# Decoding two tiles' experts inside the expert loop, with own pools for the first product's operands

## The chip, the cores and the metric

The kernel runs on one core of a Trainium2 chip. The metric is the device time of one execution in microseconds (us), lower is better. A core has engines that run their own instruction lists in order and meet by semaphores: TensorE (PE, matrix products), VectorE (DVE), ScalarE (ACT), GpSimd (POOL) and SyncE (SP, which here only issues transfers). Transfers are moved by 16 DMA engines, whichever engine issued them.

## The reference, cut to what matters

One encoder layer over 1024 tokens of width 1024: attention, a layer norm, and then a layer of product-key experts (PEER), to which the change belongs:

```python
q   = (x @ w_q).reshape(n, 8, 2, 128)
sc  = einsum('nhpc,hpkc->nhpk', q, sub_keys)          # 8 heads x 2 halves x 128 keys
s_top, i_top = top_k(sc, 16)
cand     = s_top[:, :, 0, :, None] + s_top[:, :, 1, None, :]
cand_idx = i_top[:, :, 0, :, None] * 128 + i_top[:, :, 1, None, :]
fs, fpos = top_k(cand, 16);  eidx = take(cand_idx, fpos);  g = softmax(fs)
h   = einsum('cd,chkd->chk', x, u[eidx])              # 16384 experts, one row of u and of v each
out = einsum('chk,chkd->cd', gelu(h) * g, v[eidx])
x   = layer_norm(alpha * x + out)
```

Every token uses 8 x 16 = 128 of 16384 experts.

## The kernel before, in words

The 1024 tokens are eight tiles of 128. Attention and routing take the tiles in pairs: `route(pr)`, for tiles 2pr and 2pr+1, forms the scores on PE, takes each half's best 16 on DVE (`top16`) and then calls `decode`, some 150 small DVE instructions per tile that turn 2 x 16 scores per head into 16 expert numbers and 16 gate values.

From there two ways lead to the output. Tiles 0 to 4 (`ND` = 5) go the dense way: their gates are written as a matrix over all 16384 experts, and h and the output are dense products. For tiles 0 and 1 the gates are added into memory by 256 indirect transfers that POOL issues one after the other (`scatter`, L165; memory tensor `gs`). For tiles 2 to 4 `build` makes them: DVE writes one-hot rows (`pi`, `qj`, L602 and L606), ACT scales `qj` (L611), PE multiplies them (L615), ACT copies the product into a staging tile (L616) and SP writes that to memory tensor `gd` (L617). Tiles 5 to 7 go the gathering way: POOL fetches for one expert slot the 128 rows of u and v that 128 tokens need (`uv`, L656); DVE multiplies and sums them with the tokens (`xg`, L658), ACT applies gelu, DVE multiplies with the gate (`hh`, L663) and adds the scaled v row to `acc` (L668). There are 384 such gathers.

After the routing (`late.close()` frees its buffers) comes the expert loop of 128 blocks of 128 experts. Per block `hstage` loads a block of u, splits it into a rounded part and a rest (`uh` on ACT, `ul` on DVE), makes h in two halves of 24 products each (L91 to L93), applies gelu (`gl`), multiplies with the gates (`gt`, L722), splits that (`ah`, `al`) and splits a block of v (`vh`, `vl`). The output is summed in PSUM for tiles 0 to 2 (`po`, 18 products per block) and, every second block, flushed for tiles 3 and 4 (`fl`, `facc`). The loop also feeds the gathers: three per block, four blocks' worth ahead.

The order of every engine's list is fixed when the program is built: a scheduler places instructions of different stages beside each other where data and buffers allow. A pool of tiles that opens later can lie on memory that an earlier pool has given back; its first writer then waits for the last users of what lay there.

Of the kernel before, what the change touches and what calls it, by code (L numbers as in the profile page):

```python
# [11 lines left out]
F32 = mybir.dt.float32  # L12
F32R = mybir.dt.float32r
BF16 = mybir.dt.bfloat16
I32 = mybir.dt.int32
U32 = mybir.dt.uint32
# [3 lines left out]
PSUM = bass.MemoryType.PSUM  # L20

P = 128
S = 1024
D = 1024
KT = D // P
# [6 lines left out]
TOPK = 16  # L32
# [7 lines left out]
DN = ND * P  # L40
# [17 lines left out]
def trunk(ctx, tc, x, xt, wqk, wo, gn, sink, biasa, biasb, ln, wq, keyst, uv, ut, vt, out):  # L58
    nc = tc.nc
    f = lambda ap: ap.bitcast(F32)  # L60
# [20 lines left out]
    def load_ln(g):  # L81
        for i in range(2):
            nc.scalar.dma_start(lnt[:, i, :], bcast_rows(ln[2 * g + i], D))
# [89 lines left out]
            new.append(st.ins)  # L173
        added[t, h] = new

    def decode(idx, g, sv, iv, pool, t=None):
        s2 = sv.rearrange("p (h two) k -> p h two k", two=2)
        fi = pool.tile([P, 8, 2, TOPK], F32, name="fi", bufs=1)
        nc.vector.tensor_copy(fi, iv.rearrange("p (h two) k -> p h two k", two=2))
        cv = pool.tile([P, 8, NCAND], F32, name="cv", bufs=1)  # L180
        for a in range(8):
            w = WIDTHS[a]
            nc.vector.tensor_tensor(cv[:, :, OFFS[a]:OFFS[a] + w], s2[:, :, 1, 0:w],
                                    s2[:, :, 0, a:a + 1].to_broadcast([P, 8, w]), OP.add)
        nc.vector.tensor_tensor(cv[:, :, NCAND - 8:], s2[:, :, 0, 8:16],
                                s2[:, :, 1, 0:1].to_broadcast([P, 8, 8]), OP.add)
        fs = pool.tile([P, 8, TOPK], F32, name="fs", bufs=1)
        pos = pool.tile([P, 8, TOPK], U32, name="pos", bufs=1)
        for h in range(8):
            top16(fs[:, h, :], pos[:, h, :], cv[:, h, :], pool, NCAND)  # L190
        pf = pool.tile([P, 8, TOPK], F32, name="pf", bufs=1)
        nc.vector.tensor_copy(pf, pos)
        dlt = pool.tile([P, 8, TOPK - 1], F32, name="dlt", bufs=1)
        nc.vector.tensor_sub(dlt, fi[:, :, 0, 1:], fi[:, :, 0, 0:TOPK - 1])
        nc.vector.scalar_tensor_tensor(dlt, dlt, 64.0, wrow[:, None, :].to_broadcast([P, 8, TOPK - 1]),
                                       op0=OP.mult, op1=OP.add)
        big = pool.tile([P, 8, 8, TOPK], F32, name="big", bufs=1)
        ef = pool.tile([P, 8, TOPK], F32, name="ef", bufs=1)
        e2 = pool.tile([P, 8, TOPK], F32, name="e2", bufs=1)
        bsum = big.rearrange("p a h k -> p h k a")  # L200
        nc.vector.tensor_scalar(big[:, 0, :, :], fi[:, :, 0, 0:1].to_broadcast([P, 8, TOPK]), 64.0, None, op0=OP.mult)
        for a in range(1, TOPK):
            nc.vector.scalar_tensor_tensor(big[:, a % 8, :, :], pf, START[a] - 0.5,
                                           dlt[:, :, a - 1:a].to_broadcast([P, 8, TOPK]), op0=OP.is_ge, op1=OP.mult)
            if a % 8 == 7:
                nc.vector.tensor_reduce(ef if a == 7 else e2, bsum, AX.X, OP.add)
        nc.vector.tensor_add(ef, ef, e2)
        ei = pool.tile([P, 2, 8 * TOPK], I32, name="ei", bufs=1)
        e0 = ef.rearrange("p h k -> p (h k)")
        nc.vector.tensor_copy(ei[:, 0, :], e0)  # L210
        nc.vector.tensor_scalar(ei[:, 1, :], ei[:, 0, :], 63, None, op0=OP.bitwise_and)
        nc.vector.tensor_scalar(ei[:, 0, :], ei[:, 0, :], 6, 7, op0=OP.logical_shift_right, op1=OP.logical_shift_left)
        of = pool.tile([P, 2, 8, TOPK], F32, name="of", bufs=1)
        nc.vector.tensor_copy(of.rearrange("p a h k -> p a (h k)"), ei)
        nc.vector.tensor_sub(pf, pf, of[:, 1])
        for b in range(TOPK):
            nc.vector.scalar_tensor_tensor(big[:, b % 8, :, :], pf, float(b),
                                           fi[:, :, 1, b:b + 1].to_broadcast([P, 8, TOPK]),
                                           op0=OP.is_equal, op1=OP.mult)
            if b % 8 == 7:  # L220
                nc.vector.tensor_reduce(ef if b == 7 else e2, bsum, AX.X, OP.add)
        nc.vector.tensor_add(ef, ef, e2)
        if t is None:
            nc.vector.tensor_add(idx.rearrange("p (h k) -> p h k", h=8), ef, of[:, 0])
        else:
            nc.vector.tensor_scalar(ef, ef, float(P * GC), base[:, t:t + 1], op0=OP.mult, op1=OP.add)
            nc.vector.scalar_tensor_tensor(idx.rearrange("p (h k) -> p h k", h=8), of[:, 0], GC / P, ef,
                                           op0=OP.mult, op1=OP.add)
        gv = g.rearrange("p (h k) -> p h k", h=8)
        nc.vector.tensor_tensor(gv, fs, fs[:, :, 0:1].to_broadcast([P, 8, TOPK]), OP.subtract)  # L230
        nc.scalar.activation(g, g, AF.Exp)
        gs = pool.tile([P, 8], F32, name="gs")
        nc.vector.tensor_reduce(gs, gv, AX.X, OP.add)
        nc.vector.reciprocal(gs, gs)
        nc.vector.tensor_mul(gv, gv, gs[:, :, None].to_broadcast([P, 8, TOPK]))


    late = ExitStack()

    with ExitStack() as att:  # L240
# [278 lines left out]
        def route(pr):  # L519
# [14 lines left out]
                    nc.scalar.dma_start(xd[1, :, :, t * P:(t + 1) * P], f(tl[:, :, tok]))  # L534
            stop_ = {t: rs.tile([P, 16, TOPK], F32, name="stop", bufs=4) for t in tiles}
            itop = {t: rs.tile([P, 16, TOPK], U32, name="itop", bufs=4) for t in tiles}
            for c in range(16):
                if pr == 0 and c % 4 == 0:
                    raw = r1.tile([P, P, GC], F32, name="stage").rearrange("p a c -> p (a c)")
# [26 lines left out]
                    top16(stop_[t][:, c, :], itop[t][:, c, :], sc[:, n, :], rs, P)  # L566
            dense = []
            for t in tiles:
                if t >= ND:
                    decode(eidx[t], gate[t], stop_[t], itop[t], rs)  # L570
                    continue
                idx = rs.tile([P, P], I32, name="idxd", bufs=4)
                g = rs.tile([P, P], F32, name="gated", bufs=4)
                decode(idx, g, stop_[t], itop[t], rs, t if t < NS else None)
                (dense if t < NS else todo).append((t, idx, g))
# [56 lines left out]
    dl = dx.tile([P, KT, DN], F32R, name="dl")  # L632
    nc.sync.dma_start(f(dh), xd[0])
    nc.sync.dma_start(f(dl), xd[1])
    x1p = ctx.enter_context(tc.tile_pool(name="x1p", bufs=2, side="right"))
    x1 = {}
    load_ln(1)
    gp = ctx.enter_context(tc.tile_pool(name="gp", bufs=GBUF, side="right"))
    ga = ctx.enter_context(tc.tile_pool(name="ga", bufs=1, side="right"))
    sm = ctx.enter_context(tc.tile_pool(name="sm", bufs=2))  # L640
# [37 lines left out]
    def pump(n):  # L678
        while n > 0 and done[0] < total:
            next(gen)  # L680
            done[0] += 1
            n -= 1

    dn = ctx.enter_context(tc.tile_pool(name="dn", bufs=2))
    ph = ctx.enter_context(tc.tile_pool(name="ph", bufs=1, space=PSUM))
    RES = 3
# [17 lines left out]
        if NS < ND:  # L704
            nc.sync.dma_start(gt[g][:, ns:], gd[:, :, sl, :].rearrange("q j i c -> j q i c"))

    def hstage(e, pend):
        raw = dn.tile([P, KT, P], F32, name="raw", bufs=3)
        nc.sync.dma_start(raw, ut[e])
        uh = dn.tile([P, KT, P], F32R, name="uh")  # L710
        ul = dn.tile([P, KT, P], F32R, name="ul")
        split(uh, ul, raw)
        gl = dn.tile([P, DN], F32, name="gl")
        for j, (o, n) in enumerate(hch):
            ps = ph.tile([P, 512], F32, name="h")
            for k in range(KT):
                mm3(ps[:, :n], uh[:, k, :], ul[:, k, :], dh[:, k, o:o + n], dl[:, k, o:o + n], k == 0, k == KT - 1)
            nc.scalar.activation(gl[:, o:o + n], ps[:, :n], AF.Gelu)  # L718
            if j == (e == ne - 1) and pend is not None:
                vres(*pend)  # L720
        glv = gl.rearrange("p (q c) -> p q c", c=GC)
        nc.vector.tensor_mul(glv, glv, gt[e // EG][:, :, e % EG, :])  # L722
        ah = dn.tile([P, DN], F32R, name="ah", bufs=3)
        al = dn.tile([P, DN], F32R, name="al", bufs=3)
        split(ah, al, gl)
        raw = dn.tile([P, D], F32, name="raw", bufs=3)
        nc.sync.dma_start(raw, vt[e * P:(e + 1) * P, :])
        vh = dn.tile([P, D], F32R, name="vh", bufs=3)
        vl = dn.tile([P, D], F32R, name="vl", bufs=3)
        split(vh, vl, raw)  # L730
        return ah, al, vh, vl
# [15 lines left out]
    def vflush(e, a):  # L747
        prev.append(a)
        if len(prev) == 2:
            for c in range(RES, ND):  # L750
                acc = facc[c - RES]
                if e == 1:
                    xr[c] = dn.tile([P, D], F32, name="raw", bufs=3)
                    nc.scalar.dma_start(xr[c], xs[c])
                for j in range(2):
                    ps = ph.tile([P, 512], F32, name="fl")
# [10 lines left out]

    fed = 0
    pend = None
    load_g(0)  # L770
    for e in range(ne):
        if e % EG == 0 and e + EG < ne:
            load_g(e // EG + 1)
        a = hstage(e, pend)
        if pend is not None:
            vflush(*pend)
        pend = (e, a)
        while fed < min(total, total * (e + 4) // ne):
            pump(1)
            fed += 1  # L780
    vres(*pend)
# [81 lines left out]
```

## Time and profile before

| | |
|---|---|
| median of 3 runs | 2982.5 us (2979.24 to 2985.24) |
| the profiled execution | 2985.32 us |
| its span in the trace | 2981.6 us |
| PE busy | 2733.9 us, 92% |
| DVE busy | 2408.1 us, 81% |
| ACT busy, POOL busy | 1202.3 us (40%), 1065.1 us (36%) |
| mean granted TensorE clock | 0.961 of full speed |

The span is what the trace covers; 3.7 us of the execution lie outside it. The stage up to about 1110 us is attention and routing, the expert loop runs from about 1133 to 2960 us, and the layer norms of the last tiles end it. A busy share is an average over the stages; the change touches mostly the place where one stage passes into the other.

### The profile page before, as it was taken

The page shows a single profiled execution, that of the slowest core. Times are in us where ns is not written, and L with a number is a line of the kernel's source. Part 1 is how long each engine was busy: PE and PEld are TensorE (multiplying, and loading weights), DVE is VectorE, ACT ScalarE, POOL GpSimd, SP SyncE. Part 2 cuts the span into 40 slices and gives each one's busy share as a digit, 9 for nine tenths or more (in the row PEclk, how much of TensorE's full clock was granted, in tenths as well). Part 3 has the DMA queues.
Part 4 walks back from the last instruction along what each step waited for, and adds up shares of the span by engine and source line. Part 5 has one row for each costly group of instructions (what it writes and reads, how often), then busy time and mean ns, then how long its engine had stood idle before and what let it go on. Part 6 is the DMA issues. An engine that isn't in the chain of part 4 may idle for free.

```text
span 2981.6 us, 43327 instructions
## 1 busy us (share of the span) xinstructions
PE 2733.9 (92%) x15569; PEld 2357.3 (79%) x15569; DVE 2408.1 (81%) x5427; ACT 1202.3 (40%) x2486; POOL 1065.1 (36%) x732
## 2 busy tenths in 40 slices
PE   6887899897997867999999999999999999999996
PEld 4776577575785766888998899898888898988885
DVE  2344267887979988898998989999989999998965
ACT  2343154342786762333333343333333333333332
POOL 1111001078888881333333323333333333333300
PEclk8998989898997988999999999999999999999998
DMA  7688598897977767988998989998998898998851
GB/s 233 200 271 269 177 322 296 260 262 180 267 223 221 220 161 265 348 331 324 353 331 332 332 329 335 336 347 334 330 344 327 321 353 322 342 349 332 329 210 46
DMA packets 384886, 854.37 MB, mean 287 GB/s; under 512 B 83616, under 2 KB 243360, under 8 KB 333728
## 3 DMA queue, kind: packets, MB, share of 16 engines
q0 software_dynamic: 124224, 433.43, 41.3%
q1 hardware_dynamic: 230816, 388.82, 38.5%
q10 hardware_dynamic: 29632, 29.37, 3.1%
q8 instruction: 122, 2.00, 0.3%
q14 instruction: 92, 0.75, 0.1%
HBM read 765.21 MB, written 86.11 MB: 286 GB/s over the span
## 4 chain that ended last, share of the span: by engine, by line
PE 48%; DVE 5%; DMA 4%; issue 3%; ACT 2%; POOL 1%; SPq 0%; ACTq 0%; POOLq 0%; DVEq 0%
PE h L91 9%; PE h L92 8%; PE h L93 8%; PE po L736 5%; PE po L737 5%; PE po L738 5%; PE fl L737 3%; PE fl L736 3%; PE fl L738 3%; DMA uv<-in_uv_dram,eidx 2%; DMA raw<-in_ut_dram 2%; DVE uv L658 1%; DVE acc L668 1%; POOL uv L656 1%; DVE vl L87 1%
## 5 line engine op out<-in xcount | busy, mean ns | idle before, releaser
L656 POOL DMA_INDIRECT uv<-in_uv_dram,eidx x384 | 570.4, 1486 | 1162.5 <-DVE acc L668 688.5
L91 PE MATMUL h<-dh,uh 128*128 128x320 f32 x2048 | 641.3, 313 | 49.0 <-ACT uh L86 25.6
L93 PE MATMUL h<-dh,ul 128*128 128x320 f32 x2048 | 634.6, 310 | 0.8 <-DVE ul L87 0.8
L92 PE MATMUL h<-dl,uh 128*128 128x320 f32 x2048 | 634.1, 310 | 0.0
L658 DVE SCALAR_TENSOR_TENSOR uv<-uv,xg 128x1024 f32<-128x1024 f32 x384 | 467.4, 1218 | 43.1 <-DMA uv<-in_uv_dram,eidx 37.3
L165 POOL DMA_INDIRECT gs<-gated,idxd x256 | 434.9, 1699 | 171.3 <-DMA qlo<-wqd 87.0
L668 DVE SCALAR_TENSOR_TENSOR acc<-uv,hh,acc 128x1024 f32<-128x1024 f32 x381 | 487.6, 1280 | 4.3
L91 PEld LDWEIGHTS h<-dh,uh 128*128 128x128 f32 x2048 | 385.7, 188 | 83.7 <-ACT gl L718 48.6
L92 PEld LDWEIGHTS h<-dl,uh 128*128 128x128 f32 x2048 | 385.9, 188 | 10.9
L93 PEld LDWEIGHTS h<-dh,ul 128*128 128x128 f32 x2048 | 385.7, 188 | 4.9 <-DVE ul L87 1.5
L736 PE MATMUL po<-vh,ah 128*128 128x512 f32 x768 | 288.2, 391 | 1.5 <-ACT ah L86 1.5
L737 PE MATMUL po<-vl,ah 128*128 128x512 f32 x768 | 287.8, 391 | 0.0
L662 ACT ACTIVATE hh<-hh 128x1 f32<-128x1 f32 x384 | 77.6, 202 | 476.3 <-DVE uv L658 474.9
L738 PE MATMUL po<-vh,al 128*128 128x512 f32 x768 | 260.8, 391 | 0.0
L764 ACT COPY fl<-fl 128x512 f32<-128x512 f32 x252 | 147.1, 584 | 278.7 <-PE fl L738 278.5
L765 DVE TENSOR_TENSOR facc<-facc,fl 128x512 f32<-128x512 f32 x252 | 172.6, 685 | 72.8 <-ACT fl L764 72.6
L718 ACT ACTIVATE gl<-h 128x320 f32<-128x320 f32 x256 | 111.4, 435 | 254.5 <-PE h L93 244.4
L736 PE MATMUL fl<-vh,ah 128*128 128x512 f32 x512 | 201.8, 394 | 3.0 <-ACT fl L764 3.0
L737 PE MATMUL fl<-vl,ah 128*128 128x512 f32 x512 | 201.9, 394 | 0.0
L738 PE MATMUL fl<-vh,al 128*128 128x512 f32 x512 | 199.6, 390 | 0.0
L87 DVE TENSOR_TENSOR ul<-raw,uh 128x1024 fp32r<-128x1024 f32 x128 | 156.1, 1220 | 52.6 <-ACT uh L86 51.7
L86 ACT CAST uh<-raw 128x1024 fp32r<-128x1024 f32 x128 | 134.2, 1049 | 116.8 <-DMA raw<-in_ut_dram 60.7
(201 smaller groups left out, 5389.2 us busy)
## 6 DMA issues: line engine op xcount, KB each, us to landing
raw<-in_ut_dram SPq DMA_DIRECT2D x128, 512.0 KB
raw<-in_vt_dram SPq DMA_DIRECT2D x128, 512.0 KB
qhi<-wqd SPq DMA_DIRECT2D x48, 512.0 KB
qlo<-wqd SPq DMA_DIRECT2D x48, 512.0 KB
gd<-stage SPq DMA_DIRECT2D x12, 2048.0 KB
gt<-gd SPq DMA_DIRECT2D x32, 768.0 KB
wraw<-in_wqk_dram SPq DMA_DIRECT2D x36, 512.0 KB
bt<-in_biasb_dram SPq DMA_DIRECT2D x64, 288.0 KB
```

What stands on the lines that cost most here:

```text
L87: nc.vector.tensor_sub(lo, raw, f(hi))
L91: nc.tensor.matmul(ps, wh, mh, start=first, stop=False)
L92: nc.tensor.matmul(ps, wh, ml, start=False, stop=False)
L93: nc.tensor.matmul(ps, wl, mh, start=False, stop=last)
L165: st = nc.gpsimd.indirect_dma_start(out=gs, out_offset=bass.IndirectOffsetOnAxis(ap=idx[:, k:k + 1], axis=0), in_=g[:, k:k + 1], in_offset ...
L656: nc.gpsimd.indirect_dma_start(out=u, out_offset=None, in_=uv, in_offset=bass.IndirectOffsetOnAxis(ap=eidx[t][:, k:k + 1], axis=0))
L658: nc.vector.scalar_tensor_tensor(u[:, 0:D], u[:, 0:D], 1.0, x1[t], op0=OP.mult, op1=OP.mult, accum_out=hh[:, k:k + 1])
L668: nc.vector.scalar_tensor_tensor(acc, u[:, D:], hh[:, k:k + 1], acc, op0=OP.mult, op1=OP.add)
L736: nc.tensor.matmul(ps, ah[:, cs], vh[:, js], start=first, stop=False)
L737: nc.tensor.matmul(ps, ah[:, cs], vl[:, js], start=False, stop=False)
L738: nc.tensor.matmul(ps, al[:, cs], vh[:, js], start=False, stop=last)
L765: nc.vector.tensor_add(acc[:, j, :], acc[:, j, :], fl)
```

## The change

Four things are changed together.

- `decode` becomes a generator, `decode_steps`, which yields after each of its eight `top16` and after every four steps of its sums: 16 steps per tile. Tiles 0 to 5 run it through at once as before. For tiles 6 and 7 `route(3)` leaves it out and holds their scores; two steps per block run in the first 16 blocks of the expert loop. Their scores lie in the first half of the constant tile `lnt` (a layer norm's scale), their scratch in its second half and in a small new tile `side`; `load_ln(1)`, which fills `lnt` for the second layer norm, moves behind the last step.
- The loaded u and v blocks (`raw`), `uh`, `ul` and `gl` get an own pool, `du`, and the sums of h an own PSUM pool, `hb`. Both open before the pools of the gathers and of the rest of the loop.
- The first block of u is loaded before the first gates, and the following gates are loaded after the block's `hstage` instead of before it.
- The gathers are fed as 2e+4 up to block 17 and then evenly up to block 124, instead of three per block.

```diff
@@ decode
-    def decode(idx, g, sv, iv, pool, t=None):
+    def decode(*args):
+        for _ in decode_steps(*args):
+            pass
+
+    def decode_steps(idx, g, sv, iv, pool, t=None):
...
             top16(fs[:, h, :], pos[:, h, :], cv[:, h, :], pool, NCAND)
+            yield
@@ route
+            if pr == 3:
+                for n, t in enumerate(tiles):
+                    stop_[t] = carve(lflat, 512 * n, [P, 16, TOPK])
+                    itop[t] = carve(lflat, 512 * n + 256, [P, 16, TOPK], U32)
+                    held[t] = stop_[t], itop[t]
...
             for t in tiles:
+                if t in held:
+                    continue
@@ behind late.close()
     nc.sync.dma_start(f(dh), xd[0])
     nc.sync.dma_start(f(dl), xd[1])
+    du = ctx.enter_context(tc.tile_pool(name="du", bufs=2))
+    hb = ctx.enter_context(tc.tile_pool(name="hb", bufs=1, space=PSUM))
     x1p = ctx.enter_context(tc.tile_pool(name="x1p", bufs=2, side="right"))
     x1 = {}
-    load_ln(1)
...
+    side = dx.tile([P, 9 * P], F32, name="side")
+
+    def held_decodes():
+        for t in sorted(held):
+            yield from decode_steps(eidx[t], gate[t], *held[t], Carve(side))
+
+    hd = held_decodes()
@@ hstage
-    def hstage(e, pend):
-        raw = dn.tile([P, KT, P], F32, name="raw", bufs=3)
+    def load_u(e):
+        raw = du.tile([P, KT, P], F32, name="raw", bufs=3)
         nc.sync.dma_start(raw, ut[e])
-        uh = dn.tile([P, KT, P], F32R, name="uh")
-        ul = dn.tile([P, KT, P], F32R, name="ul")
+        return raw
+
+    def hstage(e, pend, raw):
+        uh = du.tile([P, KT, P], F32R, name="uh")
+        ul = du.tile([P, KT, P], F32R, name="ul")
         split(uh, ul, raw)
-        gl = dn.tile([P, DN], F32, name="gl")
+        gl = du.tile([P, DN], F32, name="gl")
         for j, (o, n) in enumerate(hch):
-            ps = ph.tile([P, 512], F32, name="h")
+            ps = hb.tile([P, 512], F32, name="h")
...
-        raw = dn.tile([P, D], F32, name="raw", bufs=3)
+        raw = du.tile([P, D], F32, name="raw", bufs=3)
@@ the loop
+    first = load_u(0)
     load_g(0)
     for e in range(ne):
+        a = hstage(e, pend, load_u(e) if e else first)
         if e % EG == 0 and e + EG < ne:
             load_g(e // EG + 1)
-        a = hstage(e, pend)
         if pend is not None:
             vflush(*pend)
         pend = (e, a)
-        while fed < min(total, total * (e + 4) // ne):
+        for _ in range(2 if hd is not None else 0):
+            if next(hd, 0) == 0:
+                hd = None
+                load_ln(1)
+                break
+        while fed < min(total, 2 * e + 4 if e < 18 else 40 + (total - 40) * (e - 17) // (ne - 21)):
             pump(1)
             fed += 1
```

How the scheduler then lays out the lists is not to be read from the diff. Three places of it follow. Line numbers in the pieces of the changed kernel are its own: L640 and L644 make `pi` and `qj`, L649 scales `qj`, L653 multiplies, L654 copies into the staging tile, L689 loads `xg`, L695 gathers, L697 multiplies a gathered row, L771 is `gl` with the gates, L785 to L787 are the output products.

On PE, the passage from the last gate product into the expert loop, before (`pr_9832` is the last product of `build`, `h_11466` the first half block of h):

```order
L615 MATMUL pr_9818<-pi_9819,qj_9821 128x128 x4
L615 MATMUL pr_9832<-pi_9833,qj_9835 128x128 x4
L91 MATMUL h_11466<-dh_11424,uh_11461 128x320
L92 MATMUL h_11466<-dl_11425,uh_11461 128x320
L93 MATMUL h_11466<-dh_11424,ul_11462 128x320
```

and now:

```order
L653 MATMUL pr_9818<-pi_9819,qj_9821 128x128 x4
L653 MATMUL pr_9832<-pi_9833,qj_9835 128x128 x4
L785 MATMUL po0_11209<-vh_11283,ah_11277 128x512
L786 MATMUL po0_11209<-vl_11284,ah_11277 128x512
L785 MATMUL po1_11210<-vh_11283,ah_11277 128x512
```

Five half blocks of h (120 products, for blocks 0, 1 and half of 2) now stand far ahead, before the first score products of `route(3)`, so that output products follow the last gate product at once.

On ACT, with the semaphores each instruction waits for, the loads of `xg` before (a wait on DMASW is one for transfers that POOL issued):

```order
L718 ACTIVATE gl_11465<-h_11492 128x320 [waits PE_49]
L754 DMA raw_11817<-xs_94 128x1024 [waits DMAHW1_49,DVE_49]
L86 CAST ah_11519<-gl_11465 128x640 [waits DVE_49]
L718 ACTIVATE gl_11611<-h_11612 128x320 [waits PE_49]
L650 DMA xg_11530<-xs_94 128x1024 [waits DMASW4_49,DMASW3_49,DMASW5_49,DMASW2_49,DMASW6_49,DMASW1_49,DMASW7_49,DMASW0_49,DVE_49]
L650 DMA xg_16529<-xs_94 128x1024
```

and now (`stage_9733` is the last staging tile that `build` fills, `qj_9793` to `qj_9835` its last four groups):

```order
L649 ACTIVATE qj_9779<-qj_9779,tt_9389 128x128 x3
L689 DMA xg_11311<-xs_94 128x1024 [waits DMASW4_49,DMASW5_49,DMASW3_49,DMASW6_49,DMASW2_49,DMASW7_49,DMASW1_49,DMAHW1_49,DMASW0_49,DVE_49]
L654 COPY stage_9733<-pr_9734 128x4x128 [waits DMAHW0_49]
L654 COPY stage_9733<-pr_9748 128x4x128
L689 DMA xg_17150<-xs_94 128x1024 [waits DMAHW2_49]
L654 COPY stage_9733<-pr_9762 128x4x128 [waits PE_49]
L649 ACTIVATE qj_9793<-qj_9793,tt_9389 128x128 [waits DVE_49]
L649 ACTIVATE qj_9793<-qj_9793,tt_9389 128x128 x3
L654 COPY stage_9733<-pr_9776 128x4x128 [waits PE_49]
```

The load, with its wait for the transfers that POOL issued, has moved from behind the first one and a half blocks of gelu to a place ahead of all eight copies of the last staging tile.

On DVE, what stands around the first gathered row (`uv_11533`), before; the rows of `decode` above it are the end of tile 7's:

```order
L217 SCALAR_TENSOR_TENSOR big_11347<-pf_11342,fi_11280 128x128 x8
L221 TENSOR_REDUCE e2_11349<-big_11347 128x128
L222 TENSOR_TENSOR ef_11348<-ef_11348,e2_11349 128x128
L224 TENSOR_TENSOR eidx7_104<-ef_11348,of_11373 128x128
L722 TENSOR_TENSOR gl_11611<-gl_11611,gt_11453 128x640
L87 TENSOR_TENSOR ul_11856<-raw_11853,uh_11855 128x1024
L87 TENSOR_TENSOR al_11684<-gl_11611,ah_11683 128x640
L658 SCALAR_TENSOR_TENSOR uv_11533,hh_11532<-uv_11533,xg_11530 128x1024
L663 TENSOR_TENSOR hh_11532<-hh_11532,gate5_105 128x1
```

and now (`side_11202` is the scratch of the held decodes):

```order
L213 TENSOR_REDUCE side_11202<-side_11202 128x128
L208 SCALAR_TENSOR_TENSOR side_11202<-lnt_89 128x128 x3
L697 SCALAR_TENSOR_TENSOR uv_11314,hh_11313<-uv_11314,xg_11311 128x1024
L208 SCALAR_TENSOR_TENSOR side_11202<-lnt_89 128x128 x5
L702 TENSOR_TENSOR hh_11313<-hh_11313,gate5_105 128x1
L213 TENSOR_REDUCE lnt_89<-side_11202 128x128
L705 TENSOR_SCALAR acc_11310<-uv_11314,hh_11313 128x1024
```

The first gathered row now stands in the middle of tile 6's decode, with most of that, all of tile 7's and every `gl` of the loop behind it; before, both decodes and the first two `gl` were ahead of it.

## Rows read from the trace of the kernel before

**Rows 1.** Stretches: length, then each engine's busy time, PE's clock, DMA.
```profile
core 0: us, PE busy (x) PEld busy (x) DVE busy (x) ACT busy (x) POOL busy (x), PEclk, DMA share, GB/s
900.00:1000.00 100.00, 73.61 (x389) 59.95 (x388) 94.41 (x375) 67.12 (x155) 84.34 (x46) 0.80 0.69 203
...
1120.00:1130.00 10.00, 0.00 (x0) 0.00 (x0) 10.00 (x41) 0.31 (x1) 0.00 (x0) 0.50 1.07 279
1170.00:2900.00 1730.00, 1709.56 (x9513) 1540.16 (x9512) 1570.22 (x2286) 621.06 (x1242) 566.58 (x380) 1.00 0.90 332
```

**Rows 2.** Waits, 1085 to 1175 us: who waited for what, total, times, longest.
```profile
POOL uv L656 <- DVE eidx L224: 42.4, 1, 42.4
PE h L91 <- ACT uh L86: 25.6, 1, 25.6
ACT gl L718 <- DVE eidx L224: 8.9, 1, 8.9
```

**Rows 3.** Chain of work that ended last: start, length, what.
```profile
1114.59 4.18 DMA gs<-gated,idxd
...
1124.24 7.67 DMA raw<-in_ut_dram
...
1138.15 1.97 DVE ef L206
...
1141.26 1.62 DVE big L203 x8
...
1159.10 3.44 DMA uv<-in_uv_dram,eidx
...
1174.06 1.14 DVE uv L658 x2
1175.21 0.74 DVE gl L722
1175.94 0.60 DVE facc L760
```

**Rows 4.** Timeline of ACT: start, length, line, operation, [idle before <-releaser].
```profile
1105.07 1.02 ACT L616 COPY stage<-pr 128x512 f32<-128x512 f32 x1
1105.89 1.27 ACT L611 ACTIVATE qj<-qj,tt 128x128 f32<-128x128 f32 x4
1107.05 1.04 ACT L616 COPY stage<-pr 128x512 f32<-128x512 f32 x1
...
1158.27 0.81 ACTq L650 DMA_DIRECT2D xg<-xs  x2
```

**Rows 5.** Timeline of DVE, small instructions and two `gl`.
```profile
1112.54 0.07 DVE L125 MATCH_VALUE_LOAD pos<-fs,cv 128x8 f32 x1
...
1112.72 0.07 DVE L125 MATCH_VALUE_LOAD pos<-fs,cv 128x8 f32 x1
...
1168.13 1.23 DVE L658 SCALAR_TENSOR_TENSOR uv<-uv,xg 128x1024 f32<-128x1024 f32 x1 [5.59 <-issue]
...
1246.87 0.81 DVE L722 TENSOR_TENSOR gl<-gl,gt 128x640 f32<-128x640 f32 x1
```

**Rows 6.** Timeline of PE: last gate products, first h, output of block 7.
```profile
1106.33 1.36 PE L615 MATMUL pr<-pi,qj 128*128 128x128 f32 x8 [0.63 <-ACT qj L611]
1133.34 0.64 PE L91 MATMUL h<-dh,uh 128*128 128x320 f32 x1 [25.65 <-ACT uh L86]
...
1149.59 0.39 PE L736 MATMUL po<-vh,ah 128*128 128x512 f32 x1
...
1252.21 0.31 PE L91 MATMUL h<-dh,uh 128*128 128x320 f32 x1
1252.35 0.39 PE L736 MATMUL po<-vh,ah 128*128 128x512 f32 x1
```

**Rows 7.** Groups by line and shape, 1170 to 2900 us: busy, mean ns.
```profile
L668 DVE SCALAR_TENSOR_TENSOR acc<-uv,hh,acc 128x1024 f32<-128x1024 f32 x381 | 487.6, 1280 | 4.3
L663 DVE TENSOR_TENSOR hh<-hh,gate 128x1 f32<-128x1 f32 x383 | 57.2, 152 | 11.0 <-ACT hh L662 11.0
```

More of the change, by code (lines that the diff above doesn't have):

```diff
@@ L204, in decode @@
                                            dlt[:, :, a - 1:a].to_broadcast([P, 8, TOPK]), op0=OP.is_ge, op1=OP.mult)
+            if a % 4 == 3:
+                yield
             if a % 8 == 7:
@@ L219, in decode @@
                                            op0=OP.is_equal, op1=OP.mult)
+            if b % 4 == 3:
+                yield
             if b % 8 == 7:
@@ L235, in decode, with carve, __init__, tile @@
         nc.vector.tensor_mul(gv, gv, gs[:, :, None].to_broadcast([P, 8, TOPK]))
+    held = {}
+    lflat = lnt.rearrange("p a d -> p (a d)")
+    def carve(flat, at, shape, dt=F32):
+        n = int(np.prod(shape[1:]))
+        ap = flat[:, at:at + n]
+        if dt is not F32:
+            ap = ap.bitcast(dt)
+        names = "abcd"[:len(shape) - 1]
+        return ap.rearrange(f"p ({' '.join(names)}) -> p {' '.join(names)}", **dict(zip(names, shape[1:])))
+    class Carve:
+        def __init__(self, side):
+            self.at = dict(fi=(lflat, 1024), fs=(lflat, 1280), pf=(lflat, 1408), dlt=(lflat, 1536), of=(lflat, 1536),
+                           pos=(lflat, 1792), ei=(lflat, 1792), e2=(lflat, 1920), cv=(side, 0), t16=(side, 512),
+                           big=(side, 0), ef=(side, 1024), gs=(side, 0))
+        def tile(self, shape, dt, name, bufs=1):
+            flat, n = self.at[name]
+            return carve(flat, n, shape, dt)
     late = ExitStack()
@@ L752, in vflush @@
                 if e == 1:
-                    xr[c] = dn.tile([P, D], F32, name="raw", bufs=3)
+                    xr[c] = du.tile([P, D], F32, name="raw", bufs=3)
                     nc.scalar.dma_start(xr[c], xs[c])
```

## The prediction

> **What bounds the kernel now.** First the stretches [rows 1]: in the loop (1170 to 2900 us) PE is busy 1709.56 of 1730 us, DVE 1570.22. PE sets the pace there, with DVE at 91%. Between 1120 and 1130 us PE does nothing and DVE is full. Next the waits around that hole [rows 2]: PE waited 25.6 us for the first `uh`, and POOL 42.4 us for tile 7's expert numbers. Then the chain [rows 3], where the reader sees why: the last scatter, issued at 1114.59, landed 4.18 us later, at 1118.8; the gate loads queue on SP; the first u block is issued at 1124.24 behind them and lands after 7.67 us. Hence the first h at 1133.34, while the last gate products began at 1106.33 [rows 6]. So the passage is tied by three things: the scatters up to 1118.8 (the change doesn't touch them), then u behind the gates, and on DVE the decode of tiles 6 and 7.
>
> The change aims at the last two. What decides is what takes their place at 1118.8.
>
> **What is removed.** The 25.6 us wait of PE: u is loaded early and five half blocks of h, 120 products, stand before `route(3)`. Between 900 and 1000 us PE is busy 73.61 of 100 us [rows 1], so they go into room there. Their cost there I put at nothing; if that cover were gone it would be 17.5 us (120 x 0.146; h products start 0.14 to 0.15 us apart, 1252.21 to 1252.35, [rows 6]), but some 18 us are to spare there, as the next step shows. The decode leaves the passage too.
>
> **What is added, step 1: ACT is held by the `xg` load.** Its first waits are all the last transfers that POOL issued: the scatters, whose index tiles lay where `xg` now lies. That they really hold ACT is in the trace: before, the same load held ACT 8.9 us until tile 7's numbers came, with a finished h waiting behind it [rows 2], and its issue shows at 1158.27 [rows 4]. There it held half a block of gelu. Now it stands ahead of the eight copies of the last staging tile and of four groups of `qj`. Before, that place was passed ahead of the copy at 1105.07 [rows 4]; now ACT stands still from about 1100 until 1118.8. Queued behind it: the copies, so the PSUM of PE's last gate products, so `pi` on DVE, so the last write to `gd`.
>
> The Trainium skill ("DMA: Bandwidth & Descriptors", Issuing engines are not separate DMA queues) says that transfers share the same 16 engines whoever starts them, and that the choice of the issuer saves only the sequencer's time, usually little. By that the load on ACT would cost its 0.81 us for two. The 8.9 us wait is what the trace shows beside it: the issuer pays the wait as well.
>
> **Step 2: the last gate products.** From 1118.8 ACT has two issues (0.81), three copies and then four groups, each a `qj` quartet and a copy. A group took 1.98 us (1105.07 to 1107.05, [rows 4]), a copy alone about 0.85: 0.8 + 2.5 + 4 x 2.0 = 11.3 us, and PE's last four products 0.7 to 1.4. They end at about 1131.5, 24 us later than before (1106.33 + 1.36).
>
> **Step 3: the first gather.** The gathers' buffers lie on memory that `build` and the scatters used: the first gather waits for the last scatters, the last `qj` and the last gate product. Issued at 1131.5, its data landed 3.44 us later by the chain [rows 3], though DVE started only 9.0 us after the issue (1159.10 to 1168.13, [rows 3, 5]), of which 5.59 us are idle time that no row explains; it may be the `xg` load issued at 1158.27, which now is early. So the first multiply starts between 1135 and 1140.5. I take 1137.5, in the middle; DVE's own small instructions ahead of it end at about 1135.
>
> **Step 4: DVE's queue behind that multiply.** DVE runs in order, and the first multiply now stands ahead of nearly all the decode and of every `gl`. From it to the `gl` of block 7 the list holds the following, at the steps from start to start that the chain shows (0.08 us under a mean, since one starts before the last has ended):
> - 26 gathered multiplies at 1.14 + 0.05 (chain 1.14, [rows 3]): 30.9
> - 23 sums into `acc` at 1.28 - 0.08 and a first one: 28.3; 25 `hh` at 0.15 [rows 7]: 3.8
> - 16 `ul` and `vl`, of a multiply's size: 16 x 1.14 = 18.2
> - 14 `gl` and `al` at 0.74: 10.4; 12 `facc` at 0.60 [rows 3]: 7.2
> - of the held decodes, 52 sums at 0.20 (1.62 for 8): 10.5; 6 reductions at 1.83 (1.97 less the overlap): 11.0 [rows 3]
> - the eight `top16` of tile 7, 40 small ones with their loads, 0.11 to 0.18 each (0.18: 1112.54 to 1112.72, [rows 5]): 6.2; some 40 others of 0.1 to 0.2: 5.0
>
> Sum 131.5 us. So `gl` of block 7 starts at 1137.5 + 131.5 = 1269, and with ACT's `ah` and DVE's `al` between them the block's output products at about 1271. Before, they started at 1252.35, PE-bound, 5.5 us after their `gl` at 1246.87 [rows 5, 6]. The difference is **+19 us**. PE doesn't set this stretch now: it has the 17.5 us of h less to do than in the 119 us of before (1133.34 to 1252.35), and 139 us for it (1131.5 to 1271). Its start of 2.5 blocks is eaten while DVE works off the decode beside the splits that every block needs.
>
> **Step 5: the rest.** From block 8 PE is the bound again and its work is the same. What is left of the decode there is covered by the feed, two gathers a block (1.19 + 1.20 + 0.15 = 2.5 us less DVE work than three). From block 18 the feed is 344/107 = 3.21 gathers a block, 0.21 x 2.5 = 0.53 us more DVE work in a block of 14.3 us (128 blocks in the 1827 us from 1133 to 2960), so 95% instead of 91%. I cost this at 0 to 5 us, hidden by PE; without that cover it would be 107 x 0.53 = 57 us. The moved load of `lnt` and the order of the gate loads are hidden: gates of block 0 would land by about 1150 (estimates from 1132.5 on: the last write to `gd`, 2 MB at the loop's 332 GB/s [rows 1], 6.3 us; then a load, 7.67 us as for u), its `gl` is due 25 us behind the first multiply, at 1163.
>
> Sum: +19 on the profiled execution's 2985.3 (2981.6 and 3.7 outside it), so 3004; that execution lies 2.8 us above the median, so 3001.5 for a median. The term's own ends: first multiply 1135 to 1140.5, the sum of step 4 good to 5 us, 0 to 5 from step 5: +11 to +32, 2994 to 3015.
>
> **Rivals.**
> - *A, it works as meant: faster.* Place: DVE between 1119 and 1270. If the `xg` wait is over by the time ACT gets there and the first gathers start soon after 1118.8, PE starts its output products at about 1128 with 17.5 us of h behind it instead of its first h at 1133.3: 5 + 17.5 = 22.5 us less, 2960. For it: PE's hole of 25.6 us really goes. Against it: even with the first multiply at 1122.5 the 131.5 us of step 4 end at 1254, so it needs step 4 to be over-counted by more than 20 us; from there it decides. A rule bears on this: the Trainium skill ("Perfetto Trace Analysis", Optimization Strategy) says that where the most contended engine changes over the program, mixing such stretches may improve it. By that the change gives the 22.5 us; the row against it is that DVE has only 9% to spare in the stretch that takes the work in.
> - *B, ACT is not held, or its hold costs nothing.* Only step 4 remains: 1122.5 + 131.5 + 2 = 1256, +4, 2986. For it: PE and DVE lists carry no scatter wait themselves. Against it: the 8.9 us row.
> - *C, the loop stalls too.* At 95% DVE work a late gather or cast costs PE time. A third of the 57 us would come to +19 beside the +19: 3020. For it: PE already loses 20 us of 1730; against it: with DVE at 91% PE hardly waits.
>
> **How the numbers follow.** The forecast has 0.57, A 0.16, B 0.15, C 0.12. The likeliest: 3001 us, its own range 2994 to 3015. The range for 8 in 10 takes in B and goes a little towards A and C: 2972 to 3016. A difference under 0.2%, 6 us, can't be told from none. Faster by more: A and a little of B, 0.18. Within: most of B, 0.12. Slower: the forecast and C, 0.70.
>
> **What would show it.** ACT idle from about 1100 to 1118.8 at the line of the `xg` load, released by the scatters; the last gate product near 1131; the first gathered multiply at 1135 to 1141; first output product near 1165 instead of 1149.59, of block 7 near 1271 instead of 1252.35; DVE without a gap between, PE with gaps that end on `al` or `ah`; from there on a constant distance to before. It is wrong if ACT passes the load before 1110, if gates or gathers come so that DVE idles after 1140, or if the distance grows or shrinks through the loop by more than 5 us.

## The result: slower by 1.4%

The changed kernel takes 3019.89 us (median of 4 runs, 3011.91 to 3033.52) against 2981.44 us before (median of 4 runs, one more than in the table ahead). The medians stand 38.5 us apart, or 1.3%; the recorded ratio of all runs is 1.0141 with a 95% interval of 1.0114 to 1.0168. The direction was forecast; the size was not: +38.5 us where +19 was said, 4 us above the stated range of 2972 to 3016.

The profiled execution has a span of 3018.9 us, 37.3 us more than before. Busy times hardly moved, and they can't show where it went (page of the changed kernel, busy us and share of the span):

```profile
PE 2737.2 (91%) x15569; PEld 2359.4 (78%) x15569; DVE 2409.7 (80%) x5427; ACT 1209.7 (40%) x2491; POOL 1060.8 (35%) x732
```

The waits of the passage do (1085 to 1200 us; who waited for what, total, times, longest), against [rows 2]:

```profile
PE po L785 <- ACT ah L86: 38.6, 1, 38.6
PE pr L653 <- ACT stage L654: 24.0, 1, 24.0
ACT stage L654 <- DMA gs<-gated,idxd: 20.1, 1, 20.1
DVE pi L640 <- PE pr L653: 17.9, 2, 17.7
POOL uv L695 <- DVE lnt L197: 15.7, 1, 15.7
DVE uv L697 <- issue: 7.0, 1, 7.0
```

PE's wait for the first `uh` (25.6 us) is gone. In its place there is a row of waits that were not there: ACT for the scatters, 20.1; PE for ACT's copy, 24.0; DVE for PE, 17.7; and PE 38.6 us for the first `ah`. ACT's timeline (start, length) names the instruction that holds it, against [rows 4]:

```profile
1094.79 1.28 ACT L649 ACTIVATE qj<-qj,tt 128x128 f32<-128x128 f32 x4 [0.63 <-DVE qj L644]
1115.78 0.34 ACTq L689 DMA_DIRECT2D xg<-xs  x1
1116.16 1.01 ACT L654 COPY stage<-pr 128x512 f32<-128x512 f32 x1 [20.10 <-DMA gs<-gated,idxd]
```

The issue itself takes 0.34 us of ACT; the 20.1 us before it are the wait that the load carries. POOL's last scatter and first gather (the profile puts the gather's wait down to a DVE instruction at 1129.4; PE's last gate product ended at 1129.5):

```profile
1112.57 1.54 POOL L165 DMA_INDIRECT gs<-gated,idxd  x1 [0.30 <-issue]
1129.77 1.05 POOL L695 DMA_INDIRECT uv<-in_uv_dram,eidx  x1 [15.65 <-DVE lnt L197]
```

PE, the end of the gate products, the first output product and the first of block 7, against [rows 6]:

```profile
1125.98 3.51 PE L653 MATMUL pr<-pi,qj 128*128 128x128 f32 x16 [1.51 <-ACT qj L649]
1168.06 0.80 PE L785 MATMUL po<-vh,ah 128*128 128x512 f32 x1 [38.56 <-ACT ah L86]
...
1280.77 0.39 PE L785 MATMUL po<-vh,ah 128*128 128x512 f32 x1
```

and DVE, the first gathered multiply, the first `gl` and that of block 7, against [rows 5]:

```profile
1140.81 1.22 DVE L697 SCALAR_TENSOR_TENSOR uv<-uv,xg 128x1024 f32<-128x1024 f32 x1 [7.04 <-issue]
...
1166.44 1.55 DVE L771 TENSOR_TENSOR gl<-gl,gt 128x640 f32<-128x640 f32 x2
...
1276.06 0.81 DVE L771 TENSOR_TENSOR gl<-gl,gt 128x640 f32<-128x640 f32 x1
```

The stretches show who set the pace (length, busy time of each engine, PE's clock), against [rows 1]:

```profile
1141.00:1166.00 25.00, 0.00 (x0) 0.00 (x0) 24.80 (x57) 3.84 (x8) 2.32 (x3) 0.50 1.04 355
1166.00:1276.00 110.00, 96.18 (x487) 83.70 (x488) 104.91 (x242) 33.44 (x64) 31.04 (x22) 0.94 0.77 281
1310.00:2940.00 1630.00, 1605.88 (x8922) 1446.33 (x8920) 1454.87 (x2115) 582.17 (x1158) 516.70 (x349) 1.00 0.88 325
```

DVE is full for 25 us in which PE does nothing, and still at 95% up to block 7, with PE at 87%; later PE is the bound again.

TensorE's clock doesn't explain the difference. Behind its hole PE runs at a granted clock of 0.50, the lower of its two levels (1.2 GHz), in both kernels: for some 5 us in the changed one (0.65 in 1170 to 1175, 1.00 from there) and some 6 us before (0.55 in 1135 to 1140, 1.00 from there).

### The profile page after: what moved, and what is told of

It reads as the page before. It is cut to its first block, busy times and chain, and to the rows that moved or that the text cites. A ratio compares the mean times of both kernels' runs of the same rounds, so it can differ in the third digit from the quotient of the medians.

```text
span 3018.9 us, 43333 instructions
## 1 busy us (share of the span) xinstructions
PE 2737.2 (91%) x15569; PEld 2359.4 (78%) x15569; DVE 2409.7 (80%) x5427; ACT 1209.7 (40%) x2491; POOL 1060.8 (35%) x732
## 4 chain that ended last, share of the span: by engine, by line
PE 44%; DVE 7%; DMA 5%; issue 4%; ACT 2%; POOL 1%; ACTq 0%; POOLq 0%; DVEq 0%; SPq 0%
PE h L91 8%; PE h L92 7%; PE h L93 7%; PE po L785 4%; PE po L786 4%; PE po L787 4%; DMA uv<-in_uv_dram,eidx 4%; PE fl L785 3%; PE fl L786 3%; PE fl L787 3%; DVE uv L697 2%; DVE acc L707 2%; DMA raw<-in_ut_dram 1%; POOL uv L695 1%; DVE vl L87 1%
## 5 line engine op out<-in xcount | busy, mean ns | idle before, releaser
L695 POOL DMA_INDIRECT uv<-in_uv_dram,eidx x384 | 565.4, 1472 | 1179.9 <-DVE acc L707 730.2
L91 PE MATMUL h<-dh,uh 128*128 128x320 f32 x2048 | 639.7, 312 | 21.8 <-ACT gl L767 19.8
L697 DVE SCALAR_TENSOR_TENSOR uv<-uv,xg 128x1024 f32<-128x1024 f32 x384 | 467.2, 1218 | 61.9 <-DMA uv<-in_uv_dram,eidx 54.2
L707 DVE SCALAR_TENSOR_TENSOR acc<-uv,hh,acc 128x1024 f32<-128x1024 f32 x381 | 487.5, 1280 | 3.6
L785 PE MATMUL po<-vh,ah 128*128 128x512 f32 x768 | 290.2, 395 | 50.2 <-ACT ah L86 49.6
L787 PE MATMUL po<-vh,al 128*128 128x512 f32 x768 | 261.6, 391 | 1.2 <-DVE al L87 1.2
L785 PE MATMUL fl<-vh,ah 128*128 128x512 f32 x512 | 203.6, 398 | 7.4 <-ACT fl L813 5.7
L785 PEld LDWEIGHTS po<-vh,ah 128*128 128x128 f32 x768 | 144.7, 189 | 81.2 <-ACT ah L86 52.5
L787 PE MATMUL fl<-vh,al 128*128 128x512 f32 x512 | 200.2, 391 | 0.0
```

Source lines behind the costliest of these rows:

```text
L91: nc.tensor.matmul(ps, wh, mh, start=first, stop=False)
L695: nc.gpsimd.indirect_dma_start(out=u, out_offset=None, in_=uv, in_offset=bass.IndirectOffsetOnAxis(ap=eidx[t][:, k:k + 1], axis=0))
L697: nc.vector.scalar_tensor_tensor(u[:, 0:D], u[:, 0:D], 1.0, x1[t], op0=OP.mult, op1=OP.mult, accum_out=hh[:, k:k + 1])
L707: nc.vector.scalar_tensor_tensor(acc, u[:, D:], hh[:, k:k + 1], acc, op0=OP.mult, op1=OP.add)
L785: nc.tensor.matmul(ps, ah[:, cs], vh[:, js], start=first, stop=False)
L787: nc.tensor.matmul(ps, al[:, cs], vh[:, js], start=False, stop=last)
```

## The experiments

The last scatter's place in the span differs between the profiled executions by up to 15 us (1103 to 1118), with the stages ahead of it. So beside the medians, the spans are compared from the start of the last scatter on. `gl` 0 and `gl` 7 are the starts of those instructions on DVE, also from there. There is one profile of each kernel, and the run with the old feed, below, shows that two nearly equal programs can differ by some 8 us in this measure too. The ratios are against the kernel before as measured beside each group: 2981.1 us for the first four kernels under the change, 2979.2 for the next three, 2982.4 for the last three.

| kernel | median us | ratio to before, 95% interval | `gl` 0 | `gl` 7 | end of span |
|---|---|---|---|---|---|
| before (profile at hand) | 2982.5 | | 32.8 | 132.3 | 1867.0 |
| the change | 3019.9 | 1.0114 to 1.0168 | 53.9 | 163.5 | 1906.4 |
| xg on POOL | 3005.6 | 1.0054 to 1.0109 | 44.8 | 157.4 | 1894.0 |
| old feed | 3027.0 | 1.0103 to 1.0158 | 50.8 | 161.4 | 1914.7 |
| pools only | 2975.6 | 0.9953 to 0.9996 | 21.8 | 126.4 | 1863.2 |
| held decodes only | 3036.5 | 1.0143 to 1.0190 | 67.0 | 177.8 | 1929.3 |
| decode first, xg on POOL | 2973.9 | 0.9958 to 0.9999 | 16.3 | 119.0 | 1855.0 |
| tile 6's decode first, old feed, xg on POOL | 2976.1 | 0.9963 to 1.0006 | 35.6 | 137.8 | 1862.7 |
| decode first, old feed, xg on POOL | 2969.7 | 0.9956 to 0.9987 | 22.8 | 122.5 | 1856.3 |
| decode first, old feed, xg on ACT | 2985.8 | 0.9997 to 1.0025 | 44.0 | 136.9 | 1871.0 |
| own u buffers | 3047.2 | 1.0206 to 1.0241 | 31.3 | 123.1 | 1934.9 |
| before, xg on POOL | 2976.2 | 0.9959 to 0.9995 | 34.6 | 135.6 | 1873.5 |

Each kernel is the changed one with the edit shown, unless said. The new order of the loads in the loop stayed in all of them and was not tested by itself.

**xg on POOL.** Is ACT's hold the cause?

```diff
-            nc.scalar.dma_start(x1[t], xs[t])
+            nc.gpsimd.dma_start(x1[t], xs[t])
```

> The changed kernel, with the loads of xg issued by POOL (behind its own scatters) instead of ACT. Theory (ACT's hold and DVE's queue add up): ACT is not held, the last gate product comes near 1108 us instead of 1129, the first gathered multiply near 1127 instead of 1140.8, and all that follows 13 us earlier: about 3006 us by the changed kernel's 3019 (3000 to 3010). Rival (only the decode's DVE work in the loop costs, the hold is covered by it): no change, 3017 to 3022. Rival (the hold is the whole loss): 2982 to 2988.

Measured 3005.6, as the theory had it. That is 14 us less by the medians, 12 from the last scatter on and 18 by the ratios (1.0141 and 1.0082): the hold is a part of the loss, not all of it. `gl` 7 comes only 6 us earlier; the other 6 us are gained behind block 7. The scheduler also moved other instructions in this run, on PE too, so the pair at the end (xg back on ACT) is the cleaner one. What is left of the loss shows in the timelines of POOL and DVE of this run:

```profile
1101.49 1.88 DVE L213 TENSOR_REDUCE side<-side 128x128 f32<-128x1024 f32 x1
...
1113.47 0.99 POOL L695 DMA_INDIRECT uv<-in_uv_dram,eidx  x1 [3.79 <-DMA gt<-gs]
...
1123.05 1.23 DVE L697 SCALAR_TENSOR_TENSOR uv<-uv,xg 128x1024 f32<-128x1024 f32 x1 [19.68 <-DMA gt<-gs]
```

The decode on DVE stops at 1103.4, queued behind a multiply whose row POOL issues only at 1113.47. That the decode itself could go on there is shown by the run with the decode first. What ACT gave back was in part spent in this wait.

**Old feed.**

```diff
-        while fed < min(total, 2 * e + 4 if e < 18 else 40 + (total - 40) * (e - 17) // (ne - 21)):
+        while fed < min(total, total * (e + 4) // ne):
```

> The changed kernel with the feed of before: three gathers a block, four blocks' worth ahead, from block 0 on. Theory (DVE sets the first eight blocks, the denser feed later costs the loop about 6 us): the first blocks get up to 15 gathers more than now, 2.5 us of DVE work each, and lose 15 to 25 us, the loop gets its 6 us back: 3025 to 3040. Rival (the denser feed later is the main loss beside the hold, the first blocks have room): about 3010.

3027.0 is in the theory's range, but the run doesn't test the feed: the edit hardly changed the lists. In the two traces PE's 15569, ACT's 2491 and POOL's 732 instructions come in the same order, and DVE's differ in 16 of 5427 places. From the last scatter to `gl` 7 both have 26 gathered multiplies, each with one read of its sum (the changed kernel, then this run; length, DVE busy time of L697, count, clock, DMA):

```profile
1112.57:1276.06 163.49, 31.80 (x52) 0.81 0.76 273
1110.68:1272.06 161.38, 31.88 (x52) 0.83 0.77 276
```

The gathers have four buffers, and most likely these set how far ahead they can run; no run varied them. So neither the theory nor the rival is decided. What the run does give is a measure of the noise: practically the same program, 7 us apart by the medians and 8 from the last scatter on, with ratios (1.0130 and 1.0141) that agree.

**Pools only.** The held decodes undone, old feed:

```diff
-            if pr == 3:
+            if False:
                 for n, t in enumerate(tiles):
...
+        while fed < min(total, total * (e + 4) // ne):
```

> The changed kernel without the held decodes (tiles 6 and 7 are decoded in route(3) as before) and with the feed of before; left of the change are the own pools and the order of the loads in the loop. Theory: the xg load stands behind the last gate copies again, ACT isn't held, two and a half blocks of h are done beside route(3), so PE's output products start near 1130 and PE sets the pace from there: 15 to 25 us below before, 2957 to 2967. Rival (the early h delays route(3), or the own pools cost the loop something): 2980 or more.

2975.6, faster than before (the interval ends at 0.9996), but by 6 us, not 15 to 25: neither the theory nor the rival. The early h works: `gl` 0 comes 11 us earlier than before, and PE's output products begin at 1131.13. From the last scatter on, it is 19 us ahead of before at `gl` 3 (56.0 against 75.3) and 1 us at `gl` 5 (100.3 against 100.9): the lead is lost in another place. SP's transfers (start, length of the issue) and the waits from 1130 to 1215 us:

```profile
1155.02 0.33 SPq L755 DMA_DIRECT2D raw<-in_ut_dram  x1
...
1164.57 0.38 SPq L746 DMA_DIRECT2D gt<-gs  x1
1165.00 0.57 SPq L751 DMA_DIRECT2D gt<-gd  x1
1165.62 18.81 SPq L755 DMA_DIRECT2D raw<-in_ut_dram  x1
```
```profile
ACT uh L86 <- DMA raw<-in_ut_dram: 22.1, 3, 10.9
PE h L91 <- ACT uh L86: 9.1, 1, 9.1
```

A u block is issued behind two gate loads, right as the first gathers begin (1163.7), its issue alone takes 18.81 us, and PE stands still for 9.1 us. That is about half of the lead that is lost there; the other half stays open.

**Held decodes only.** The pools back, held decodes and feed kept:

```diff
-    du = ctx.enter_context(tc.tile_pool(name="du", bufs=2))
-    hb = ctx.enter_context(tc.tile_pool(name="hb", bufs=1, space=PSUM))
...
+    du, hb = dn, ph
```

> The changed kernel with raw, uh, ul, gl and the sums of h back in the pools of before; left of the change are the held decodes, the feed and the order of the loads. Theory: ACT is held by the xg load as in the changed kernel, h of the first blocks is no longer ahead, but DVE sets the first eight blocks anyway and has three more ul to do there: 3017 to 3030. Rival (it is the own pools that cost, and the held decodes are harmless): 2975 to 2995.

3036.5, 6 us above the theory's range and far from the rival's: the loss is with the held decodes. Against this run the own pools give 17 us back by the medians but 8 by the ratios, whose intervals overlap: a gain, with its size near what such runs can differ by. ACT is held here too, ahead of a `qj`:

```profile
1115.88 0.82 ACTq L687 DMA_DIRECT2D xg<-xs  x2
1116.81 1.28 ACT L649 ACTIVATE qj<-qj,tt 128x128 f32<-128x128 f32 x4 [25.37 <-issue]
```

The hold comes with the held decodes, then: it is here without the own pools, and in the run with pools only the load is issued at 1162.86, behind the first `gl`. Why is argued, not shown: before, `xg` waited for tile 7's numbers as well; with the decode's scratch moved elsewhere only the scatters hold it, and the scheduler can put the load further up ACT's list.

**Decode first.** If the order on DVE is the rest of the loss, the same instructions in another order must recover it. Scratch and scores stay where the change put them; the held decodes are written ahead of the loop, and the first four multiplies follow them; xg on POOL:

```diff
+                    if t == ND and k < GBUF:
+                        tc.add_manual_dep(mul.ins, last_decode[-1].ins.name, SYNC, reason="decode first")
...
+    for _ in hd:
+        pass
+    load_ln(1)
...
-        for _ in range(2 if hd is not None else 0):
-            if next(hd, 0) == 0:
-                hd = None
-                load_ln(1)
-                break
```

> The changed kernel with xg's loads on POOL, the held decodes written ahead of the loop, and the multiplies of the first four gathers made to follow the last decode instruction of tile 7; feed as in the changed kernel. In the run with xg on POOL alone DVE stood idle 19.7 us at the first multiply (1103.4 to 1123.1 us) with decode work queued behind it. Theory (what is left of the loss is this order on DVE): the idle time is filled with decode, gl of block 7 comes about 20 us earlier than its 1260.6, and the time falls from 3005.6 to 2980 to 2990. Rival (the loss is the amount of DVE work beside the loop, wherever it stands): 3000 to 3010.

2973.9, 6 us below the theory's range: 32 us less than with xg on POOL alone, 31 by the ratios, 39 from the last scatter on. DVE's work in the whole run is the same (busy 2412.8 us against 2408.2), so its amount was not the cause; its order was. But the theory's reason, the idle time, is the smaller part of it. From the last scatter to `gl` 7, xg on POOL and then this run (length, busy time of PE, PEld, DVE, ACT and POOL, clock, DMA):

```profile
1103.18:1260.60 157.42, 98.29 (x512) 85.93 (x513) 131.97 (x302) 37.71 (x74) 46.08 (x31) 0.83 0.78 276
1118.26:1237.24 118.98, 91.52 (x467) 80.62 (x468) 102.10 (x245) 32.20 (x58) 26.52 (x21) 0.87 0.73 259
```

`gl` 7 comes 38.4 us earlier. DVE idles 8.6 us less up to it and is busy 29.9 us less: 14 gathered multiplies stand ahead of `gl` 7 instead of 26, and 14 sums into `acc` instead of 24. The edit makes the multiplies wait for the end of the decode, and the `gl` of the first blocks pass them. The two effects were not separated.

With only tile 6's decode first (`last_decode[-2]`) and the old feed:

> As the one before, but the first four multiplies follow tile 6's decode only, and the feed is three per block as before the change. Theory: DVE's idle time at the first multiply is filled in part (tile 6's rest is some 17 us), tile 7's decode still stands between gl of the first blocks: between the two others, 2985 to 3000. Rival (amount, not order): 3000 to 3027, as the changed kernel with the old feed.

2976.1; `gl` 0 and `gl` 7 lie between the two, as the theory had it, the total 9 us below its range. Here 23 multiplies stand ahead of `gl` 7, and yet the end, from the last scatter on, is 31 us earlier than with xg on POOL alone: the place of `gl` 7 by itself doesn't set the end. And both first, with the old feed:

> As the run with the decode first, with the feed of three gathers per block from the start. Theory: once the decode is over by about 1150 us DVE has room for three gathers a block, so no more is lost in the first blocks, and the loop keeps 4 points of DVE more to spare: 0 to 6 us below the run with the decode first, 2976 to 2988. Rival (the old feed costs 7 us as it did in the changed kernel): 2990 or more.

2969.7, the lowest median: 0.9972 of before, interval 0.9956 to 0.9987. It is 4 us below the run with the decode first, inside the 0 to 6 of the theory, though below the absolute range. But again the feed hardly changed the lists (POOL's order is the same, DVE's differs in 38 of 5427 places), and the 4 us are within what the runs can tell: the intervals overlap, and from the last scatter on it is 1 us slower.

**xg back on ACT.** The last kernel, with `nc.scalar` for the load again:

> The run with the decode first and the old feed (2969.7 us), with xg's loads back on ACT. Theory (the hold of ACT costs by itself, since the last gate products, the last write to gd and with it the first gates and gl wait for it): ACT stands still some 20 us again, first output products at 12 to 15 us later from the last scatter on, 2979 to 2985. Rival (the hold costs only through the first gather, which no longer is waited for): 2967 to 2973.

2985.8, 16 us slower by the medians (14.7 from the last scatter on, 12 by the ratios, whose intervals don't overlap), with PE's order the same in all but 12 of 15569 places and the hold and its successors back:

```profile
ACT stage L657 <- DMA gs<-gated,idxd: 19.3, 1, 19.3
DVE pi L643 <- PE pr L656: 16.8, 1, 16.8
```

So the hold costs by itself, though no gather is waited for here. The way leads over the last gate products: DVE stands 16.8 us at `pi` with decode queued behind it, and `gl` 0, which needs the gates, comes 21 us later.

**Own u buffers.** A try for more, on the fastest kernel: its u blocks come late while blocks of v hold the three buffers.

```diff
-        raw = du.tile([P, KT, P], F32, name="raw", bufs=3)
+        raw = du.tile([P, KT, P], F32, name="rawu", bufs=2)
...
-        raw = du.tile([P, D], F32, name="raw", bufs=3)
+        raw = du.tile([P, D], F32, name="raw", bufs=1)
...
-                    xr[c] = du.tile([P, D], F32, name="raw", bufs=3)
+                    xr[c] = du.tile([P, D], F32, name="raw", bufs=1)
```

> The run with the decode first and the old feed, with two own buffers for raw blocks of u and one for raw blocks of v instead of three for both. In that run PE still loses some 9 us between 1140 and 1180 us, where ACT waits up to 10.7 us for a u block while the DMA engines are busy 18% of the time. Theory (u is late because blocks of v hold the buffers): u comes ahead, 5 to 10 us less, 2960 to 2966. Rival (one buffer for v makes vh and vl late in the loop): slower, 2975 to 3000.

3047.2, the rival's way and 47 us beyond its range. `gl` 7 comes as early as in the fastest kernel (123.1 against 122.5); all is lost in the loop. There (1300 to 2900 us) PE waits 59.3 us for `gl` (17.7 in the fastest kernel) and ACT 205.7 us for PE to free `uh` (48.3), and blocks of v come late:

```profile
ACT uh L86 <- PE h L92: 205.7, 104, 6.7
PE h L91 <- ACT gl L772: 59.3, 64, 2.5
ACT vh L86 <- DMA raw<-in_vt_dram: 50.9, 23, 6.8
```

**The kernel before, with xg on POOL.**

> The kernel before, with xg's loads on POOL. There ACT was held 8.9 us by this load with a finished half block of h behind it. Theory: PE had work besides, and POOL's first gather waits for the same expert numbers, so little changes: 2977 to 2984. Rival (the 8.9 us were paid by PE): 2970 to 2975.

2976.2, between the two; the interval (0.9959 to 0.9995) just excludes no change, but from the last scatter on this profile is 6.5 us slower than before's. What the 8.9 us of [rows 2] cost is not settled by it.

## Why the prediction missed, by its own steps

The steps that failed are 3 and 4, together 9.8 us too small up to block 7, and step 5, put at 0 to 5 us, where this trace lost 8.9.

- **The removed wait**: right. No PE wait for `uh` is left. A cost of the early h ahead of the passage doesn't show: the last scatter starts 2 us earlier than before; but that place varies by up to 15 us, so a smaller cost isn't excluded.
- **Step 1, ACT held**: right, 20.1 us with the chain of successors as named; two experiments price it at 12 to 18 us. The 8.9 us row that it leaned on was a wait for tile 7's numbers ([rows 2]); that the scatters hold ACT is shown only by the runs. Of the Trainium skill's rule ("DMA: Bandwidth & Descriptors", Issuing engines are not separate DMA queues) the 0.34 us of the issue agree; the 20.1 us of the wait it leaves out, and they decide.
- **Step 2**: right. The gate products were said to end at 1131.5 and end at 1129.5, in both cases 16.9 us behind the start of the last scatter.
- **Step 3**: first multiply at 1137.5, measured 1140.8, past the late end of what was given: 11.0 us after the gather's issue, where [rows 3, 5] have 9.0. The `xg` load isn't the reason; it was issued 25 us before the multiply. Between the gather's issue and the multiply the DMA engines move 330 GB/s, 3.6 MB in 11 us, and four gathers of 1 MB each (128 rows of u and v, 8 KB) are issued from 1129.77 on; so the first row probably lands together with the next three (an estimate from these numbers, not shown by itself). **+3.3**.

```profile
1129.80:1140.80 11.00, 0.00 (x0) 0.00 (x0) 3.90 (x11) 3.65 (x4) 3.87 (x4) 0.62 0.85 330
```

- **Step 4, DVE's list**: 131.5 us, measured 135.3 (1140.81 to 1276.06). The instructions were summed well (130 us busy); DVE idled 5.1 us of 1166 to 1276, which the sum had as none: **+3.8**. And the output products of block 7 came 4.7 us behind their `gl`, not 2: **+2.7**. That makes +28.4 at block 7 instead of +19 (1280.77 against 1252.35).
- **Step 5, the rest at 0 to 5 us**: from block 7 to the end another **8.9** us were lost (28.4 to 37.3). `gl` of blocks 8 to 24 lies 29 to 33 us behind before, then 28 to 40 to the end. PE's idle share in the loop is 24.1 us of 1630 against 19.2 of the 1620 from 1280 to 2900 before. It isn't a denser feed, for there was none: from `gl` 18 to `gl` 120 DVE runs 3.18 gathered multiplies a block, and before it ran 3.20, not the 3 that the code asks for. DVE is busy 89% of the loop (1454.87 of 1630), not 95%, and was at 91% before (1469.93 of 1620):

```profile
1280.00:2900.00 1620.00, 1600.84 (x8907) 1442.24 (x8906) 1469.93 (x2140) 582.41 (x1165) 531.57 (x356) 1.00 0.90 331
```

From `gl` 7 to the end the changed kernel needs 1742.9 us, the one before 1734.7. The run with the old feed, nearly the same program, needs 1753.3, and held decodes only 1751.5; xg on POOL needs 1736.6 and decode first 1736.0. So among these the loss shows only with both the hold and the spread decode, and its size is known to some 10 us only. One place of it is in the trace: a u block, issued behind two gate loads, comes late, and PE waits (ACT, then PE):

```profile
1804.92 1.04 ACT L86 CAST uh<-raw 128x1024 fp32r<-128x1024 f32 x1 [9.33 <-DMA raw<-in_ut_dram]
1806.64 0.79 PE L785 MATMUL po<-vh,ah 128*128 128x512 f32 x1 [5.13 <-ACT ah L86]
```

Why such waits cost the changed kernel more than the others is open.

So the mechanism of the passage stood, and its sum was too small at three joints by some 3 to 4 us each and in the loop, in this trace, by 9 where 0 to 5 were allowed; the forecast counted a full engine as an engine without gaps, and let the passage end at block 7. Its own sign of being wrong came true: the distance to before grew through the loop by more than 5 us.

Rival C (3020 us) was met in number, by luck: it wanted 19 us from a denser feed in the loop, and that feed didn't come about. Rival B fell with the 20.1 us and their price.

Rival A, that it works as meant, was priced at 2960 and given 0.16, because "the 131.5 us" would have to be over-counted. That reading was too narrow. The 131.5 us were counted well for the list as it stood; they were a matter of its order. With the decode first, and the hold gone, `gl` 7 comes 119.0 us after the last scatter instead of 163.5, largely because 12 gathered multiplies no longer stand ahead of it. The rule of the Trainium skill beside it ("Perfetto Trace Analysis", Optimization Strategy) is not refuted by these runs: what cost was where the list put the first multiplies. But none of them shows the mixing itself to gain: the best with held decodes have ratios of 0.9972 and 0.9978, pools only, without them, 0.9974.

## What to carry to other kernels

- A load carries its waits to the engine that issues it. When a change frees memory, look where the loads that waited for it now stand, and what is queued behind them on the issuing engine.
- On an engine that runs in order, work that is moved beside a loop costs more when an instruction that waits for a transfer stands ahead of it. Sum its list from the first such wait on, see which instructions ahead of the loop's own could as well stand behind, and compare with the sum in that order.
- Compare profiles from a common event ahead of the change, not only from the start of the span, and have two runs of the same program for the noise: here 7 to 8 us.
- Before reading an experiment, see in the two traces whether its edit changed the order of the lists. A feed that the code states as denser was none.

## What the runs showed that was not expected

The issue of a 512 KB load can hold SP for long, in the kernel before as well. Of the 31 loads of a block that stand right behind two gate loads, 21 before and 24 in the changed kernel take over 3 us to issue (median of the 31: 4.7 and 4.2 us); with pools only, one among the first gathers took 18.81. The other loads of blocks take 0.33 us in the median. Why was not tested.

Two buffers for blocks of u and one for v, in place of three shared, cost 78 us. Whether v's single buffer does it or u's missing third was not separated.
